# A gated-linear-attention encoder layer: the first sweep reads its tokens from a transposed copy of the input, and the norm factor of each token is multiplied in behind the matrix products

## The chip, the cores and the metric

The kernel runs on one NeuronCore of a Trainium2 chip. The metric is the device time of one execution in microseconds (us). Five engines work from queues of their own, each strictly in order: TensorE (PE in the profile; PEld is its weight load), VectorE (DVE), ScalarE (ACT), GpSimd (POOL) and SyncE (SP), which here only issues DMA transfers. They wait for each other through semaphores.

## The reference

With 2048 tokens of width 1024 and depth 1, one layer is computed: a norm over the tokens, a gated linear attention (GLA) mixer, a residual, a second norm, a feed-forward part with a short convolution, a residual, and a last norm. What the change touches is the first line and the projection behind it:

```python
def rms_normalize(x):
    y = xf * lax.rsqrt(jnp.mean(xf * xf, axis=-1, keepdims=True) + EPS)
...
h = rmsnorm(x, mix_norm_w[i])          # rms_normalize(x) * w
...
proj = h @ w_in                        # 1024 x 3088
q, k, v, r, glr = jnp.split(proj, ...)
log_a = jax.nn.log_sigmoid(glr @ w_gate2 + b_gate) / GLA_TAU
...                                    # scan over chunks of 64 tokens
o = rms_normalize(o) * norm_w * silu(r)
y = o @ w_out
x = x + y
x = x + conv_ffn(rmsnorm(x, ffn_norm_w), w_up, conv_w, conv_b, w_down)
return rmsnorm(x, final_norm_w)
```

The factor `rsqrt(mean(x*x) + EPS)` is one number for each token. A product `h @ w` is linear in the token's row, so this number can be applied to the row or to the result.

## The kernel before, in words

All large products run in float32 on PE as three matmuls of split operands (a high part, which ACT makes by a cast, and a low part, which DVE makes by a subtraction): `split` at L186, `mm3p` at L172. Products of 2x2 blocks are done with seven multiplications instead of eight (OPS, PORD at L81 to L83: p1, p5, p6, p2, p7, p3, p4 in the order in which they run). Tokens come in 16 tiles of 128; a unit takes two of them.

Four sweeps run over the eight units: R (the gate r of the mixer and the rank-16 decay gate), A and B (q, k, v of two heads each, and the scan), Y (the output projection). Then follow the two parts of the feed-forward stage. PE's time is filled by these one after the other; the first sweep, R, lasts until 228 us of the profiled span.

In sweep R the tokens must be normalised and transposed, since a matmul contracts over the partition dimension. `load_x` (L372) brings a tile of 128 tokens x 1024 into a ring of four raw buffers. `norm_x` (L379) squares it on ACT with a running sum (`rstd_of`, L204), takes the power -1/2 on POOL and multiplies the tile by this factor and the norm's weights on DVE (L383). `blocks_x` (L394) transposes the tile by eight PE matmuls with an identity (L401) into two PSUM banks and copies them to SBUF as blocks `hb` (L406; DVE, for tiles 2 and 3 ACT). `diff` makes the block differences `ht`. `prep_row` and `split_row` (L360, L426) split each of the seven operands and store it for the later sweeps (`h1d`).

`first_pair` (L908) does unit 0 by hand while weights still arrive: eight plain products (`product`, L1004) and the gate's small matmuls (`gate_plain`). `unit` (L1060) does the others. A unit's product p1 goes to a PSUM bank, ACT copies it out (`cp_R`, L1147), and p6, then p7 and p4 are accumulated onto the same bank; between them the partial sums are read out: p6 is copied like p1, p7 is added on DVE to the copy of p5 (L1091), and p4 is copied on ACT (L1163). So p6 can't begin before p1 is copied, p7 not before p6 is, p4 not before p7 is read. The decay gate's 32 rows (`gate_mm`, `gate_rows`) are multiplied by `w_gate2` with the bias as two further rows of ones (L567), and ACT takes softplus straight from PSUM (L569). `later_do` and `wevents` set the place of such work by a count of PE microseconds (`adv`). Behind this the framework orders each engine's instructions itself, so the order of a stream is not that of the source.

Of the kernel before, what the change touches and what calls it, by code (L numbers as in the profile page):

```python
# [16 lines left out]
P = 128  # L17
# [8 lines left out]
def hybrid_kernel(  # L26
    ctx: ExitStack,
    tc: tile.TileContext,
    x: bass.AP,
    mix_norm_w: bass.AP,  # L30
    ffn_norm_w: bass.AP,
# [340 lines left out]
    def load_x(t, name):  # L372
        xt = raw_tile([P, D], f"{name}_{t}")
        nc.sync.dma_start(xt, x[t * P:(t + 1) * P, :])
        return xt

    xin = {}

    def norm_x(t):  # L379
        xt = xin[t]  # L380
        junk = gp.tile([P, 1024], BF16, tag="cp", name=f"junk_{t}", bufs=4)
        rstd = rstd_of(xt, D, f"a{t}", junk, "a", nc.gpsimd if t < 4 else None)
        nc.vector.scalar_tensor_tensor(xt, xt, rstd, rp["nw"], op0=ALU.mult, op1=ALU.mult)  # L383

# [9 lines left out]
    def blocks_x(t):  # L394
        xt = xin.pop(t)
        bs = []
        for k in range(2):
            pt = aux_ps(f"pt_a{t}_{k}")
            for i in range(HK):
                kt = HK * k + i  # L400
                nc.tensor.transpose(pt[:, i * P:(i + 1) * P], xt[:, kt * P:(kt + 1) * P], ident)  # L401
# [4 lines left out]
            (nc.scalar.copy if t in (2, 3) else nc.vector.tensor_copy)(b, pt)  # L406
# [57 lines left out]
    def gate_weights():  # L464

        GR = 2 * RANK
        rp["wg"] = wg = rp["p"].tile([P, 2, KT, GR], F32R, name="wg")
        rp["wgx"] = wgx = rp["p"].tile([P, 2, KT, GR], F32R, name="wgx")
        graw = rp["p"].tile([P, 512], F32, tag="s2k", name="graw", bufs=SB)
        gv = graw[:, :KT * RANK].rearrange("p (a b) -> p a b", b=RANK)  # L470
        nc.sync.dma_start(gv, wv[:, :, OR + H * DV:OR + H * DV + RANK])
        nc.gpsimd.memset(f32(wg[:, 1, :, RANK:GR]), 0.0)
        nc.vector.tensor_copy(wg[:, 0, :, :RANK], gv)
        nc.vector.tensor_copy(wg[:, 1, :, :RANK], gv)
        nc.vector.tensor_sub(wg[:, 0, :, RANK:GR], gv, f32(wg[:, 0, :, :RANK]))
        nc.gpsimd.memset(f32(wgx[:, 1, :, RANK:GR]), 0.0)

        def others():

            gx_ = graw[:, KT * RANK:2 * KT * RANK].rearrange("p (a b) -> p a b", b=RANK)  # L480
            nc.vector.tensor_add(gx_[:, :HK], gv[:, :HK], gv[:, HK:])
            nc.vector.tensor_scalar(gx_[:, HK:], gv[:, :HK], -1.0, 0.0, op0=ALU.mult, op1=ALU.add)
            nc.vector.tensor_copy(wgx[:, 0, :, :RANK], gx_)
            nc.vector.tensor_copy(wgx[:, 1, :, :RANK], gx_)
            nc.vector.tensor_sub(wgx[:, 0, :, RANK:GR], gx_, f32(wgx[:, 0, :, :RANK]))

        later_do(24.0, others)

    def gate_weights2():
# [4 lines left out]
        for i in range(6):  # L494
            nc.sync.dma_start(w2raw[i * RANK:(i + 1) * RANK, :], w_gate2)
        for i in range(2):
            nc.sync.dma_start(w2raw[96 + i:97 + i, :], b_gate)
        def parts():
            nc.vector.tensor_copy(w2s[0:98, :], w2raw[0:98, :])
            for r in (slice(64, 96), slice(96, 98)):  # L500
                nc.vector.tensor_sub(w2s[r, :], w2raw[r, :], f32(w2s[r, :]))
            nc.vector.tensor_copy(w2s[96:97, :], w2raw[96:97, :])

        later_do(44.0, parts)
        rp["gstk"] = rp["p"].tile([P, T], F32R, name="gstk")
        nc.gpsimd.memset(f32(rp["gstk"][96:98, :]), 1.0)

# [49 lines left out]
    def gates(b, t0, t1, t2):  # L557
# [6 lines left out]
        def softplus(half):  # L564
            for tt in (2 * half, 2 * half + 1):
                pz = aux_ps(f"pz_{b}_{tt}")
                nc.tensor.matmul(pz, rp["gstk"][0:98, tt * P:(tt + 1) * P], rp["w2s"][0:98, :], start=True, stop=True)  # L567
                e = s2k(f"e_{b}_{tt}")
                nc.scalar.activation(e, pz, AF.Softplus, scale=-1.0)  # L569
                es.append(e)  # L570
# [339 lines left out]
    def first_pair():  # L910
# [42 lines left out]
        def weight(slot, ij, key=None):  # L953
# [50 lines left out]
        def product(i, jj, k):  # L1004
# [6 lines left out]
            if jj == 1:  # L1011
                t = out_tile(f"o{i}{k}_{ps_}_{j}")
                nc.scalar.copy(t, bank[i, k])
                nc.sync.dma_start(rd[k][i], t)
# [16 lines left out]
        need_raw[0, 1] = a12  # L1031
        product(1, 0, 0)
        norm_x(2)
        norm_x(3)
        product(1, 0, 1)
        weight("p2", (0, 1), "p2")
        product(1, 1, 0)
        gate_plain(j, 1, 0, *h[1, 0])
        blocks_x(2)
        blocks_x(3)  # L1040
        product(1, 1, 1)
        gate_plain(j, 1, 1, *h[1, 1])
        done["rows"] = len(PORD)
        prep_rows(len(PORD) + 1)
        sum5()
        product(0, 1, 0)
        prep_rows(len(PORD) + 2)
        sum6()
        product(0, 1, 1)
        later_do(22.0, diffs)  # L1050
        for t in (4, 5):
            xin[t] = load_x(t, "x")
        heapq.heappush(wevents, (clock["now"] + 1.0, next(seq), sum7))
# [10 lines left out]
    def unit(ps_, j):  # L1064
# [15 lines left out]
        if ps_ == "R":  # L1080
            if j + 2 < NP:
                for t in (e + 4, d + 4):
                    xin[t] = load_x(t, "x")
            if j + 1 < NP:
                for i, t in enumerate((e + 2, d + 2)):
                    norm_x(t)
                    later_do(TX[i], lambda t=t: blocks_x(t))

        def out(src, other, name):
            t = out_tile(f"{name}_{ps_}_{j}")  # L1090
            add(t, src, other)  # L1091
            return t
# [5 lines left out]
        for i, o in enumerate(PORD):  # L1098
# [46 lines left out]
            if o in ("p1", "p5", "p6"):  # L1145
                keep[o] = cp_tile(f"c{o}_{ps_}_{j}")
                nc.scalar.copy(keep[o], a)  # L1147
            elif o == "p2":
                o11 = out(a, keep["p1"], "o11")
            elif o == "p7":  # L1150
                o22 = out(a, keep["p5"], "o22")
            elif o == "p3":
                o12 = out(a, keep["p6"], "o12")
            if ps_ == "R":
# [6 lines left out]
                elif o == "p4":  # L1161
                    o21 = out_tile(f"o21_{ps_}_{j}")
                    nc.scalar.copy(o21, a)  # L1163
                    nc.sync.dma_start(rd[e][1], o21)
            else:
# [11 lines left out]
                elif o == "p4":  # L1177
                    scan[n]["v"] = scan_v(g, e, a)
                scan_slot(4 * i + 4)
# [263 lines left out]
    rp["h"] = rp["hctx"].enter_context(tc.tile_pool(name="rh", bufs=1, side="right"))  # L1443
    xin[0] = load_x(0, "x")
    rp["nw"] = rp["h"].tile([P, D], F32, name="nw_mix")
    nc.sync.dma_start(rp["nw"], mix_norm_w.partition_broadcast(P))
    xin[1] = load_x(1, "x")
    first_pair()
# [94 lines left out]
_INS = [  # L1543
    "x", "mix_norm_w", "ffn_norm_w", "final_norm_w",
    "gla_w_in", "gla_w_gate2", "gla_b_gate", "gla_norm_w", "gla_w_out",
# [26 lines left out]
```

## Time and profile before

| | us |
|---|---|
| time, median of 3 runs | 2183.61 (2178.07 to 2184.76) |
| span of the profiled execution (first to last instruction) | 2176.4 |
| sweep R in that span, to the first product of sweep A | 0 to 228.4 |
| the two feed-forward stages | 852 to 2176.4 |

The page gives the span of the profiled execution and no time beside it; what lies around a span (7.2 us from the median's side) is taken as the same before and after. A row of the profile names a line, an engine, an operation and its tiles (output <- inputs), then a count, the busy time, the mean time of one in ns and the idle time before it. A row of a timeline gives start, duration, engine, line and operation.

### The profile page before, as it was taken

What the parts mean: (1) busy time and instruction counts of PE and PEld (TensorE: products, weight loads), DVE (VectorE), ACT (ScalarE), POOL (GpSimd) and SP (SyncE); (2) the same over time, 40 slices, a digit from 0 to 9 for tenths busy, and PEclk for the clock granted to TensorE, in tenths of its full rate; (3) what the DMA queues carried; (4) which work ended last, traced back from release to release, by engine and by line L of the source; (5) the groups of instructions that cost most, each with busy time, mean ns of one, the idle gap of its engine ahead of it and who ended that gap; (6) DMA issues with size and microseconds to landing.
All of it is one profiled execution on the core that took longest, in us unless ns stands there. A gap on an engine that the chain in (4) does not pass through costs nothing.

```text
span 2176.4 us, 28914 instructions
## 1 busy us (share of the span) xinstructions
PE 2086.0 (96%) x9832; PEld 1730.6 (80%) x9832; DVE 1648.3 (76%) x2168; ACT 1104.3 (51%) x2024; POOL 734.9 (34%) x606
## 2 busy tenths in 40 slices
PE   7999999989998999799999998999999999999998
PEld 5788788878887887677888777888888877888886
DVE  8756888798888663778899776988888776457564
ACT  5555756665565775444554453554445533333342
POOL 2000011111111002456666554666565444037010
PEclk9999999999999999999999999999999999999999
DMA  6646684578557999654453458242424567254453
GB/s 219 223 165 211 213 297 137 159 229 298 178 195 251 323 344 365 207 163 131 146 184 102 146 177 291 88 131 76 139 77 124 187 247 269 97 184 160 141 182 113
DMA packets 305124, 411.76 MB, mean 189 GB/s; under 512 B 23742, under 2 KB 160110, under 8 KB 304976
## 3 DMA queue, kind: packets, MB, share of 16 engines
q1 hardware_dynamic: 267440, 346.99, 48.2%
q10 hardware_dynamic: 37536, 62.93, 8.6%
q8 instruction: 77, 1.26, 0.2%
q14 instruction: 71, 0.58, 0.1%
HBM read 266.70 MB, written 143.13 MB: 188 GB/s over the span
## 4 chain that ended last, share of the span: by engine, by line
PE 65%; DVE 13%; DMA 10%; issue 6%; ACT 2%; POOL 2%; SPq 0%; ACTq 0%; DVEq 0%; POOLq 0%
PE pd_p L180 5%; PE pd_p L181 5%; PE pd_p L179 5%; PE ua L179 5%; PE ua L180 5%; PE ua L181 5%; DVE t L1255 4%; DMA h_p<-hd_p 2%; PE uc L179 2%; PE uc L181 2%; PE uc L180 2%; PE mp_Y L180 2%; PE mp_Y L181 2%; PE mp_Y L179 2%; PE mp_R L179 2%
## 5 line engine op out<-in xcount | busy, mean ns | idle before, releaser
L179 PE MATMUL ua<-h_p,uw_p 128*128 128x512 f32 x704 | 279.0, 396 | 28.0 <-ACT c L1237 23.2
L1255 DVE SCALAR_TENSOR_TENSOR t<-u,cw,t 128x1024 f32<-128x1024 f32 x176 | 270.4, 1542 | 10.3 <-ACT t L1253 9.1
L180 PE MATMUL ua<-h_p,uw_p 128*128 128x512 f32 x704 | 277.7, 394 | 0.0
L181 PE MATMUL ua<-h_p,uw_p 128*128 128x512 f32 x704 | 277.2, 394 | 0.0
L180 PE MATMUL pd_p<-dw_p,da 128*128 128x512 f32 x616 | 240.7, 391 | 3.4 <-DVE da L189 3.4
L181 PE MATMUL pd_p<-dw_p,da 128*128 128x512 f32 x616 | 240.3, 390 | 0.0
L179 PE MATMUL pd_p<-dw_p,da 128*128 128x512 f32 x616 | 240.1, 390 | 0.0
L189 DVE TENSOR_TENSOR da<-da_p,da 128x512 fp32r<-128x512 f32 x154 | 131.4, 906 | 105.4 <-ACT da L188 105.3
L189 DVE TENSOR_TENSOR uw_p<-ur,uw_p 128x512 fp32r<-128x512 f32 x176 | 168.6, 979 | 48.8 <-ACT uw_p L188 48.4
L188 ACT CAST da<-da_p 128x512 fp32r<-128x512 f32 x154 | 85.3, 619 | 207.9 <-PE pd_p L181 149.9
L179 PEld LDWEIGHTS ua<-h_p,uw_p 128*128 128x128 f32 x704 | 134.4, 191 | 59.6 <-ACT c L1237 31.8
L188 ACT CAST uw_p<-us 128x512 fp32r<-128x512 f32 x132 | 82.1, 622 | 169.0 <-POOL us L1217 130.7
L189 DVE TENSOR_TENSOR uw_p<-us,uw_p 128x512 fp32r<-128x512 f32 x132 | 127.9, 978 | 47.8 <-ACT uw_p L188 46.8
L181 PEld LDWEIGHTS ua<-h_p,uw_p 128*128 128x128 f32 x704 | 134.5, 191 | 28.6
L180 PEld LDWEIGHTS ua<-h_p,uw_p 128*128 128x128 f32 x704 | 134.5, 191 | 27.9
L180 PEld LDWEIGHTS pd_p<-dw_p,da 128*128 128x128 f32 x616 | 116.0, 188 | 28.7 <-DVE da L189 4.7
L179 PE MATMUL uc<-h_p,uw_p 128*128 128x512 f32 x352 | 137.2, 390 | 0.9 <-DVE u L1328 0.9
L679 POOL TENSOR_TENSOR r<-r,gnw 128x512 f32<-128x512 f32 x32 | 46.9, 1466 | 268.6 <-ACT r L678 228.2
L181 PE MATMUL uc<-h_p,uw_p 128*128 128x512 f32 x352 | 136.9, 389 | 0.0
L180 PE MATMUL uc<-h_p,uw_p 128*128 128x512 f32 x352 | 136.9, 389 | 0.0
L181 PEld LDWEIGHTS pd_p<-dw_p,da 128*128 128x128 f32 x616 | 116.1, 188 | 24.1
L179 PEld LDWEIGHTS pd_p<-dw_p,da 128*128 128x128 f32 x616 | 116.1, 188 | 24.0
(278 smaller groups left out, 5474.8 us busy)
## 6 DMA issues: line engine op xcount, KB each, us to landing
ur<-in_ffn_w_up_dram SPq DMA_DIRECT2D x168, 256.0 KB, 3.7
da_p<-ad_p SPq DMA_DIRECT2D x154, 256.0 KB, 3.8
h_p<-hd_p SPq DMA_DIRECT2D x56, 512.0 KB, 8.0
ad_p<-as_p SPq DMA_DIRECT2D x88, 256.0 KB, 2.3
ad_p<-t SPq DMA_DIRECT2D x66, 256.0 KB, 3.1
x<-in_x_dram SPq DMA_DIRECT2D x32, 512.0 KB, 4.7
ch<-in_ffn_w_down_dram SPq DMA_DIRECT2D x61, 256.0 KB, 4.2
hr_A_p<-h1d_p SPq DMA_DIRECT2D x56, 256.0 KB, 3.0
```

What stands on the lines that cost most here:

```text
L179: nc.tensor.matmul(ps_ap, ah, bl, start=(first and i == 0), stop=False, **kw)
L180: nc.tensor.matmul(ps_ap, al, bh, start=False, stop=False, **kw)
L181: nc.tensor.matmul(ps_ap, ah, bh, start=False, stop=(last and i == len(pairs) - 1), **kw)
L188: nc.scalar.copy(hi, src)
L189: nc.vector.tensor_sub(lo, src, f32(hi))
L679: nc.gpsimd.tensor_mul(r, r, sp["gnw"])
L1255: nc.vector.scalar_tensor_tensor(t, u[:, k:k + TS], cw[:, k, c:c + 1], t, op0=ALU.mult, op1=ALU.add)
```

## The change

Two inputs are laid out anew on the host: `xt` holds the input tile by tile with the features on the partitions (each of 16 tiles is 128 x 2 x 512), and the norm's weights come as 128 x 8, so that feature kt*128+p lies on partition p. The blocks `hb` are now xt times the weight, one DVE multiply of 128 x 512 each with the weight broadcast along the tokens; the PE transposes, their PSUM banks and the copies out of them are gone, and so is the row norm `norm_x`.

The factor of each token goes to the result. Its square sum is taken from the rows of `x`, which are loaded once more, in halves of 128 x 512, into a single buffer `xr`: `squares` squares a half in place on ACT; then comes the load of the next half into the same buffer. After the second half POOL adds, scales and takes the power into `rs`, 128 x 16. Where a product leaves PSUM, a copy becomes an ACT activation with `rs` as its scale, an add becomes a DVE scalar_tensor_tensor, in the sweeps R, A and B. The gate's softplus is preceded by a DVE instruction that multiplies by `rs` and adds the broadcast bias `bg`; ACT then works on SBUF.

```diff
+    def load_xt(t, n=1):
+        r = raw_tile([P, 2, 512], f"xt_{t}")
+        for i in range(n):
+            ks = slice(2 * i // n, 2 * (i + 1) // n)
+            nc.sync.dma_start(r[:, ks, :], xt[t][:, ks, :])
+        return r
...
-    def norm_x(t):
-        xt = xin[t]
-        junk = gp.tile([P, 1024], BF16, tag="cp", name=f"junk_{t}", bufs=4)
-        rstd = rstd_of(xt, D, f"a{t}", junk, "a", nc.gpsimd if t < 4 else None)
-        nc.vector.scalar_tensor_tensor(xt, xt, rstd, rp["nw"], op0=ALU.mult, op1=ALU.mult)
+    def load_rows(t, i):
+        xrow[t, i] = rp["h"].tile([P, 512], F32, tag="xr", name=f"xr_{t}_{i}", bufs=1)
+        nc.sync.dma_start(xrow[t, i], x[t * P:(t + 1) * P, 512 * i:512 * (i + 1)])
...
+    def squares(t, i):
+        r = xrow.pop((t, i))
+        if i == 0:
+            sq[t] = small("ssq", f"ssq_a{t}", 2, "a")
+        nc.scalar.activation(r, r, AF.Square, accum_out=sq[t][:, i:i + 1])
+        if i == 1:
+            ssq = sq.pop(t)
+            var = small("var", f"var_a{t}", kind="a")
+            nc.gpsimd.tensor_add(var, ssq[:, 0:1], ssq[:, 1:2])
+            nc.gpsimd.tensor_scalar(var, var, 1.0 / D, EPS, op0=ALU.mult, op1=ALU.add)
+            nc.gpsimd.tensor_tensor(rs[:, t:t + 1], var, neghalf, op=ALU.pow)
...
         for k in range(2):
-            pt = aux_ps(f"pt_a{t}_{k}")
-            for i in range(HK):
-                kt = HK * k + i
-                nc.tensor.transpose(pt[:, i * P:(i + 1) * P], xt[:, kt * P:(kt + 1) * P], ident)
...
-            (nc.scalar.copy if t in (2, 3) else nc.vector.tensor_copy)(b, pt)
+            w = nwt[:, HK * k:HK * (k + 1)].unsqueeze(2).to_broadcast([P, HK, P])
+            nc.vector.tensor_tensor(b.rearrange("p (a c) -> p a c", c=P), xb[:, k, :].rearrange("p (a c) -> p a c", c=P), w, op=ALU.mult)
...
-                nc.tensor.matmul(pz, rp["gstk"][0:98, tt * P:(tt + 1) * P], rp["w2s"][0:98, :], start=True, stop=True)
+                nc.tensor.matmul(pz, rp["gstk"][0:96, tt * P:(tt + 1) * P], rp["w2s"][0:96, :], start=True, stop=True)
                 e = s2k(f"e_{b}_{tt}")
-                nc.scalar.activation(e, pz, AF.Softplus, scale=-1.0)
+                n = b * NT + tt
+                nc.vector.scalar_tensor_tensor(e, pz, rs[:, n:n + 1], rp["bg"], op0=ALU.mult, op1=ALU.add)
+                nc.scalar.activation(e, e, AF.Softplus, scale=-1.0)
...
+            nc.scalar.activation(vh, v, AF.Identity, scale=scale)
+            nc.vector.scalar_tensor_tensor(vl, v, scale, f32(vh), op0=ALU.mult, op1=ALU.subtract)
...
         fetch((0, 0))
+        xin[1] = load_xt(1, 2)
+        fetch((1, 0))
         gate_weights()
+        load_rows(0, 0)
         gate_weights2()
-        fetch((1, 0))
-        xin[2], xin[3] = load_x(2, "x"), load_x(3, "x")
         fetch((1, 1))
+        xin[2], xin[3] = load_xt(2), load_xt(3)
...
             if j + 1 < NP:
+                halves_ = [(t, i) for t in (e + 2, d + 2) for i in range(2)]
+                load_rows(*halves_[0])
+                def next_rows(n):
+                    squares(*halves_[n])
+                    if n < 3:
+                        load_rows(*halves_[n + 1])
+                for n in range(4):
+                    later_do(TSQ * (n + 1), lambda n=n: next_rows(n))
                 for i, t in enumerate((e + 2, d + 2)):
-                    norm_x(t)
                     later_do(TX[i], lambda t=t: blocks_x(t))
...
-            add(t, src, other)
+            nc.vector.scalar_tensor_tensor(t, src, rs[:, t_:t_ + 1], other, op0=ALU.mult, op1=ALU.add)
...
-                nc.scalar.copy(keep[o], a)
+                t_ = e if o == "p1" else d
+                nc.scalar.activation(keep[o], a, AF.Identity, scale=rs[:, t_:t_ + 1])
...
-                    nc.scalar.copy(o21, a)
+                    nc.scalar.activation(o21, a, AF.Identity, scale=rs[:, e:e + 1])
...
+    laid["xt"] = inputs["x"].reshape(16, 128, 2, 4, 128).transpose(0, 4, 2, 3, 1).reshape(16, 128, 2, 512)
+    laid["mix_norm_w"] = inputs["mix_norm_w"].reshape(8, 128).T
```

In `first_pair` eight calls of `next_rows` are spread between the products, and `product` copies its bank with `rs[:, k:k + 1]` as scale. TSQ is 4.8. The gate weights move to the pool that also holds `hb` and `xr`.

The change moves instructions on every engine. On PE, behind product p2 of unit 1 (`mp_R`; `pg` is the decay gate's bank), the order before is

```order
L181 MATMUL mp_R_980<-w_R_p_727,h_R_p_934 128x512
L401 MATMUL pt_a_0_993<-ident,x_869 128x128 x4
L401 MATMUL pt_a_1_1000<-ident,x_869 128x128 x4
L539 MATMUL pg_923<-h_R_p_934,wg 32x128
L540 MATMUL pg_923<-h_R_p_934,wg 32x128
```

and the order now is

```order
L181 MATMUL mp_R_944<-w_R_p_694,h_R_p_894 128x512
L182 MATMUL mp_R_944<-w_R_p_694,h_R_p_894 128x512
L183 MATMUL mp_R_944<-w_R_p_694,h_R_p_894 128x512
L560 MATMUL pg_883<-h_R_p_894,wg 32x128
L561 MATMUL pg_883<-h_R_p_894,wg 32x128
```

The eight transposes are gone there, as at all other places; nothing else of PE's order changes in sweep R but one matmul at its very start.

On ACT, in unit 3, from the copy of p1 (`cp_R_1484`, then those of p5 and p6) to the first row operand of unit 4, the order before is

```order
L1147 COPY cp_R_1484<-mp_R_1456 128x512
L188 CAST h_R_p_1505<-ht_p_1326 128x512
L1147 COPY cp_R_1503<-mp_R_1490 128x512
L188 CAST h_R_p_1523<-hb_1_1320 128x512
L1147 COPY cp_R_1521<-mp_R_1456 128x512
L188 CAST h_R_p_1566<-hb_1_1272 128x512
L208 ACTIVATE junk_1666,ssq_a_1667<-x_1432 128x1024
L208 ACTIVATE junk_1674,ssq_a_1675<-x_1434 128x1024
L188 CAST h_R_p_1613<-hb_0_1545 128x512
```

and now, over the same stretch,

```order
L1198 ACTIVATE cp_R_1418<-mp_R_1390,rs 128x512
L403 ACTIVATE xr_0_1600,ssq_a_1664<-xr_0_1600 128x512
L190 CAST h_R_p_1443<-ht_p_1265 128x512
L403 ACTIVATE xr_1_1666,ssq_a_1664<-xr_1_1666 128x512
L1198 ACTIVATE cp_R_1441<-mp_R_1424,rs 128x512
L190 CAST h_R_p_1461<-hb_1_1259 128x512
L1198 ACTIVATE cp_R_1459<-mp_R_1390,rs 128x512
L190 CAST h_R_p_1501<-hb_1_1221 128x512
L403 ACTIVATE xr_0_1711,ssq_a_1781<-xr_0_1711 128x512
L403 ACTIVATE xr_1_1783,ssq_a_1781<-xr_1_1783 128x512
L190 CAST h_R_p_1542<-hb_0_1485 128x512
```

Four squares of halves (L403) stand here, two of them ahead of the copies of p5 and p6. Counted over the whole stream of the changed kernel, squares 1 to 7 stand ahead of the copy of p1 in unit 1, 8 to 13 between there and that of unit 2, 14 to 20 up to that of unit 3, 21 to 27 up to that of unit 4; the 32nd and last stands ahead of the second row operand of unit 5.

On SP, which issues the loads of these halves (`xr`), the order now, around the 20th to 23rd of them, is

```order
L394 DMA xr_1_1529<-in_x_dram 128x512
L614 DMA ed_153<-e_3_1155 128x512
L1215 DMA rd_1_175<-o_R_1377 128x512
L394 DMA xr_0_1600<-in_x_dram 128x512
L369 DMA h1d_p_121<-hb_1_1221 128x512
L369 DMA h1d_p_123<-ht_p_1518 128x512
L394 DMA xr_1_1666<-in_x_dram 128x512
L369 DMA h1d_p_124<-ht_p_1520 128x512
L394 DMA xr_0_1711<-in_x_dram 128x512
```

The loads stand between stores of unit 2's results (`rd`), of gate factors (`ed`) and of row operands (`h1d`), each of which waits for the engine that makes it.

More of the change, by code (lines that the diff above doesn't have):

```diff
@@ L75, in hybrid_kernel @@
     TX = (10.8, 13.5)
+    TSQ = 4.8
     TS = 1024
@@ L200, in hybrid_kernel @@
     lastrow = cst.tile([P, 1], F32, name="lastrow")
+    rs = cst.tile([P, NTT], F32, name="rs")
+    nwt = cst.tile([P, KT], F32, name="nwt")
     def small(tag, name, n=1, kind=""):
@@ L466, in gate_weights @@
         GR = 2 * RANK
-        rp["wg"] = wg = rp["p"].tile([P, 2, KT, GR], F32R, name="wg")
-        rp["wgx"] = wgx = rp["p"].tile([P, 2, KT, GR], F32R, name="wgx")
+        rp["wg"] = wg = rp["h"].tile([P, 2, KT, GR], F32R, name="wg")
+        rp["wgx"] = wgx = rp["h"].tile([P, 2, KT, GR], F32R, name="wgx")
         graw = rp["p"].tile([P, 512], F32, tag="s2k", name="graw", bufs=SB)
@@ L495, in gate_weights2 @@
             nc.sync.dma_start(w2raw[i * RANK:(i + 1) * RANK, :], w_gate2)
-        for i in range(2):
-            nc.sync.dma_start(w2raw[96 + i:97 + i, :], b_gate)
+        rp["bg"] = rp["p"].tile([P, 512], F32, name="bg")
+        nc.sync.dma_start(rp["bg"], b_gate.partition_broadcast(P))
         def parts():
[L499 to L502, printed above, removed]
+            nc.vector.tensor_copy(w2s[0:96, :], w2raw[0:96, :])
+            nc.vector.tensor_sub(w2s[64:96, :], w2raw[64:96, :], f32(w2s[64:96, :]))
         later_do(44.0, parts)
         rp["gstk"] = rp["p"].tile([P, T], F32R, name="gstk")
-        nc.gpsimd.memset(f32(rp["gstk"][96:98, :]), 1.0)
     def gate_plain(j, i, c, hh, hl):
@@ L641, in scan_e, with scan_v @@
         return e
-    def scan_v(g, t, v):
+    def scan_v(g, t, v, scale=None):
         vh = sp["a"].tile([P, 512], F32R, tag=f"vh{t % 2}", name=f"vh_{g}_{t}", bufs=1 + t % 2)
         vl = sp["a"].tile([P, 512], F32R, tag=f"vl{t % 2}", name=f"vl_{g}_{t}", bufs=1 + t % 2)
-        split(vh, vl, v)
+        if scale is None:
+            split(vh, vl, v)
+        else:
+            nc.scalar.activation(vh, v, AF.Identity, scale=scale)
+            nc.vector.scalar_tensor_tensor(vl, v, scale, f32(vh), op0=ALU.mult, op1=ALU.subtract)
         return vh, vl
@@ L961, in weight, with next_rows @@
                 ready.add((ps_, key))
+        halves_ = [(t, i) for t in range(4) for i in range(2)]
+        def next_rows():
+            squares(*halves_.pop(0))
+            if halves_:
+                load_rows(*halves_[0])
         V = [(slice(None), slice(2 * k, 2 * k + 2)) for k in range(2)]
@@ L1012, in product @@
                 t = out_tile(f"o{i}{k}_{ps_}_{j}")
-                nc.scalar.copy(t, bank[i, k])
+                nc.scalar.activation(t, bank[i, k], AF.Identity, scale=rs[:, k:k + 1])
                 nc.sync.dma_start(rd[k][i], t)
@@ L1031, in first_pair @@
         need_raw[0, 1] = a12
+        next_rows()
         product(1, 0, 0)
-        norm_x(2)
-        norm_x(3)
+        next_rows()
         product(1, 0, 1)
+        next_rows()
         weight("p2", (0, 1), "p2")
+        next_rows()
         product(1, 1, 0)
@@ L1048, in first_pair @@
         sum6()
+        next_rows()
         product(0, 1, 1)
+        next_rows()
         later_do(22.0, diffs)
         for t in (4, 5):
-            xin[t] = load_x(t, "x")
+            xin[t] = load_xt(t)
         heapq.heappush(wevents, (clock["now"] + 1.0, next(seq), sum7))
@@ L1082, in unit, with out @@
                 for t in (e + 4, d + 4):
-                    xin[t] = load_x(t, "x")
+                    xin[t] = load_xt(t)
             if j + 1 < NP:
+                halves_ = [(t, i) for t in (e + 2, d + 2) for i in range(2)]
+                load_rows(*halves_[0])
+                def next_rows(n):
[4 more added lines that the diff above has]
+                    later_do(TSQ * (n + 1), lambda n=n: next_rows(n))
                 for i, t in enumerate((e + 2, d + 2)):
-                    norm_x(t)
                     later_do(TX[i], lambda t=t: blocks_x(t))
-        def out(src, other, name):
+        def out(src, other, name, t_):
             t = out_tile(f"{name}_{ps_}_{j}")
-            add(t, src, other)
+            nc.vector.scalar_tensor_tensor(t, src, rs[:, t_:t_ + 1], other, op0=ALU.mult, op1=ALU.add)
             return t
@@ L1146, in unit @@
                 keep[o] = cp_tile(f"c{o}_{ps_}_{j}")
-                nc.scalar.copy(keep[o], a)
+                t_ = e if o == "p1" else d
+                nc.scalar.activation(keep[o], a, AF.Identity, scale=rs[:, t_:t_ + 1])
             elif o == "p2":
-                o11 = out(a, keep["p1"], "o11")
+                o11 = out(a, keep["p1"], "o11", e)
             elif o == "p7":
-                o22 = out(a, keep["p5"], "o22")
+                o22 = out(a, keep["p5"], "o22", d)
             elif o == "p3":
-                o12 = out(a, keep["p6"], "o12")
+                o12 = out(a, keep["p6"], "o12", d)
             if ps_ == "R":
@@ L1443, in hybrid_kernel @@
     rp["h"] = rp["hctx"].enter_context(tc.tile_pool(name="rh", bufs=1, side="right"))
[L1444 to L1447, printed above, removed]
+    nc.sync.dma_start(nwt, mix_norm_w)
+    xin[0] = load_xt(0, 2)
     first_pair()
```

20 lines of the change are left out of this document (13 added, 7 removed).

## The prediction

> **What bounds the kernel now.** I read the page's head and its chain first, then busy time by stretches, then PE's waits inside sweep R, since all else is left as it was but for the read-outs of A and B.
>
> ```profile
> span 2176.4 us, 28914 instructions
> PE 65%; DVE 13%; DMA 10%; issue 6%; ACT 2%; POOL 2%; SPq 0%; ACTq 0%; DVEq 0%; POOLq 0%
> 0.00:18.82 18.82, 3.76 (x17) 3.23 (x17) 8.60 (x15) 8.78 (x12) 4.38 (x20) 0.98 0.81 266
> 18.82:47.70 28.88, 28.56 (x144) 23.44 (x145) 28.71 (x38) 18.69 (x30) 7.32 (x5) 0.90 0.64 218
> 47.70:228.40 180.70, 175.25 (x997) 145.11 (x996) 123.12 (x182) 99.71 (x177) 7.86 (x12) 1.00 0.59 200
> ```
>
> The three stretches are the start, unit 0 and units 1 to 7 of sweep R; the columns are length, busy time of PE, weight load, DVE, ACT and POOL, granted clock, DMA share and GB/s. From 18.82 on PE is the bound, with DVE beside it in unit 0 (28.71 of 28.88). What is taken from PE there is time, unless something becomes later than PE. ACT has room: 99.71 of 180.70.
>
> **What goes away.** The transposes, and what they cost on PE:
>
> ```profile
> L401 PE MATMUL pt_a<-ident,x 128*128 128x128 f32 x96 | 12.4, 272 | 0.0
> 36.66 1.48 PE L401 MATMUL pt_a<-ident,x 128*128 128x128 f32 x12
> 38.87 0.48 PE L179 MATMUL m_R<-w_R_p,h_R 128*128 128x512 f32 x1
> 61.55 1.03 PE L401 MATMUL pt_a<-ident,x 128*128 128x128 f32 x8
> 62.34 0.30 PE L539 MATMUL pg<-h_R_p,wg 128*32 128x128 f32 x1
> PE mp_R L179 <- ACT h_R_p L188: 1.5, 1, 1.5
> 71.75 0.68 DVE L1091 TENSOR_TENSOR o_R<-mp_R,cp_R 128x512 f32<-128x512 f32 x1
> ```
>
> The 272 ns of one overlap, so I count by starts: eight hold PE from 61.55 to 62.34, 0.79 us, and I take 0.82 with the refill behind them; a unit has sixteen, 1.65. Units 1 to 6 have them (96), 9.9 us together. In unit 0 sixteen hold PE from 36.66 to 38.87: 2.2 us. One wait of 1.5 us goes too: the row names ACT, but p4 of unit 1 needs p7 read out, and that read (71.75 to 72.43) was late on DVE behind row norms and copies that are gone.
>
> The start: before, the second matmul of the first product waits for DVE until 18.82.
>
> ```profile
> 4.64 1.06 ACT L208 ACTIVATE junk<-x 128x1024 bf16<-128x1024 f32 x1 [2.06 <-DMA x<-in_x_dram]
> 8.16 1.06 ACT L208 ACTIVATE junk<-x 128x1024 bf16<-128x1024 f32 x1 [2.37 <-DMA x<-in_x_dram]
> 11.16 1.05 ACT L188 CAST w_R_p<-ws_p 128x1024 fp32r<-128x1024 f32 x1 [0.65 <-DMA ws_p<-in_gla_w_in_dram]
> 18.82 0.80 PE L180 MATMUL m_R<-w_R_p,h_R 128*128 128x512 f32 x1 [2.50 <-DVE h_R L189]
> ```
>
> These landings give the supply: 1.5 MB (x, norm weights, x) by 8.16, 2.5 MB by 11.16, about 0.33 MB a us. Now four blocks come before DVE reaches the multiplies: its order has a sum that waits for the third weight block, and the gate weights, which now queue behind the fourth. 3 MB are in at about 12.7, the gate weights at 13.1; casts, four multiplies at 0.6 and one subtraction end at 17.1. So the start is 1.7 us earlier, no more. Without anything new in the way the sum is 1.7 + 2.2 + 9.9 + 1.5 = 15.3 us.
>
> **What is added beside PE's work.** DVE, which was full in unit 0, pays 32 multiplies of 128x512 and saves 28 copies and 16 row norms:
>
> ```profile
> L383 DVE SCALAR_TENSOR_TENSOR x<-x,rstd_a,nw_mix 128x1024 f32<-128x1024 f32 x12 | 15.3, 1283 | 7.0 <-POOL rstd_a L212 7.0
> L406 DVE COPY hb<-pt_a 128x512 f32<-128x512 f32 x24 | 15.4, 682 | 0.0
> L390 DVE TENSOR_TENSOR ht_p<-hb,hb 128x512 f32<-128x512 f32 x12 | 8.2, 683 | 0.0
> ```
>
> A multiply with a broadcast operand is in no row; the difference ht of the same size (683 ns) is nearest and I take it. In units 1 to 7 it equals the copy, so 15.3 us of norms are saved and 16 gate instructions of 0.68 (10.9) come in. In unit 0 DVE gets four multiplies (2.7) for two norms (2.6): no change. The bounds, half and double of 683 ns, move DVE by 11 us down or 22 up over a sweep in which it had 57 us of room: nothing. The scale by rs in the read-outs: ACT copies of 588 ns against some 610 for an activation (interpolated below), DVE adds of 680 with one scalar more; 85 to 96 of a kind, over sweeps in which both engines have room, so nothing on the path, and less than 0.1 us where a bank waits for one.
>
> **The new wait.** The rows of x come through one buffer. A load on SP waits for the square before it, the square for its load, and squares stand in ACT's order ahead of copies that PE waits for. So ACT can't pass a square before its load landed, and 32 of them follow each other.
>
> ```profile
> L723 ACT ACTIVATE og<-po 128x256 f32<-128x256 f32 x64 | 24.0, 381 | 22.0 <-PE po L181 18.6 <-DMA ws_B_p<-wm_B 3.5
> L208 ACT ACTIVATE junk<-x 128x1024 bf16<-128x1024 f32 x16 | 16.9, 1057 | 5.6 <-DMA x<-in_x_dram 5.4
> L208 ACT ACTIVATION_READ_ACCUMULATOR junk<-x 128x1 f32 x16 | 3.0, 189 | 0.0
> hr_A_p<-h1d_p SPq DMA_DIRECT2D x56, 256.0 KB, 3.0
> da_p<-ad_p SPq DMA_DIRECT2D x154, 256.0 KB, 3.8
> x<-in_x_dram SPq DMA_DIRECT2D x32, 512.0 KB, 4.7
> DMA to landing us min/median/max: 2.5/3.1/5.4
> ```
>
> Between 381 ns for 256 columns and 1057 for 1024 a square of 512 takes 0.61, with its read-out 0.7 (they overlap by 0.1). The last row is that of the tile r, 30 loads of 256 KB in sweeps A and B. A load of 256 KB in rows of 2 KB so takes from 2.5 (the least of these) to 4.7 (x, twice the size); hr_A is the same shape from SP, so I take its median, 3.0. One turn is 3.7 us.
>
> [...]
>
> Where the chain stands in unit 0: the second square is behind the cast of a late weight block (25.09 before; its load now goes out behind later casts), done at about 30; the fourth behind a cast that waits for DVE's sums, 39; the fifth behind a read-out that needs the factor of tile 1, that is three POOL instructions. In this stretch POOL is slow beside DVE:
>
> ```profile
> 21.10 3.10 POOL L210 TENSOR_SCALAR var_a<-ssq_a 128x1 f32<-128x1 f32 x1 [8.81 <-ACT junk L208]
> 26.48 0.45 POOL L210 TENSOR_SCALAR var_a<-ssq_a 128x1 f32<-128x1 f32 x1
> 27.02 1.53 POOL L212 TENSOR_TENSOR rstd_a<-var_a,neghalf 128x1 f32<-128x1 f32 x1
> ```
>
> 0.45 to 3.10 each, I take 1 each, 3 together: 42, then a read-out and casts, the fifth at 45, and three more turns with a cast or two bring the eighth to about 57 (54 to 60). Unit 1 then starts near 46, not at 47.7 less 5, and its p6 waits about as before.
>
> From the eighth square to the 27th are 19 turns, 70.3 us. Four places are longer: the ninth behind copies that need the factor of tile 3, 1.05; a stretch of seven ACT instructions (4.3 us) before the 15th, 1.25; the load of the 17th behind the store of a gate factor, 1.95; that of the 18th likewise, 0.6: 4.9 in all. So the 27th ends at 57 + 70.3 + 4.9 = 132.2. Behind it stand, ahead of p6 in unit 4:
>
> ```profile
> L569 ACT ACT_TABLE_LOAD x4 | 5.1, 1283 | 0.1
> L569 ACT ACTIVATE e<-pz 128x512 f32<-128x512 f32 x16 | 8.7, 598 | 0.3
> L1147 ACT COPY cp_R<-mp_R 128x512 f32<-128x512 f32 x21 | 12.4, 588 | 15.3 <-PE mp_R L181 14.7 <-issue 0.6
> 133.39 0.59 ACT L1147 COPY cp_R<-mp_R 128x512 f32<-128x512 f32 x1 [0.19 <-PE mp_R L181]
> ```
>
> A table load, two softplus and the copy: 1.3 + 1.2 + 0.6 = 3.1, so p6 starts at 135.3. Before, p5 of unit 4 has ended at 133.4 (the last row) and p6 follows at once. The change is therefore 1.9 us **behind** at that point: all that PE saved by then, some 10 us, is waited away. Behind it only five squares are left, and no copy of the next units stands behind one that is late; the transposes of units 4, 5 and 6 are then a plain gain, 3 x 1.65 = 4.95. Net: 3.05 us earlier at the end of R.
>
> Against the profiled execution's own time this is 2176.4 - 3.05; what lies around the span stays, so from the median 2183.6 I get **2180.6**. Sweeps A, B and what follows keep their order but for a few neighbours that change places, and I count nothing there.
>
> **The rivals.** (1) The loads are quick, at 2.5 us: a turn of 3.2 takes 9.5 us off the 19, the 27th square ends at 122.7, and the gain is 12.5: 2171.1; near the 15.3 of the ceiling. For it: loads of r have reached it, and sweep R's DMA share is only 0.59. Against it: the median of these loads is 3.1. [...] (2) Slower: the loads take 3.8, as da_p of the same size does. A turn is then 4.5, p6 of unit 4 starts 15.2 later, 12.2 us behind before at the end: 2195.8. It decides from a load of 3.16 on (no gain) and is a loss of more than 6.5 us from 3.5 on. For it: R gets 8 MB more to load, and SP's order puts stores that wait ahead of loads. Against it: hr_A at 3.0. With 4.7 it would be 17 more. (3) The change does not do what it says, because DVE in unit 0 or POOL's three instructions hold the start: each us of the eighth square is a us of the end; 60 instead of 57 gives 2183.6, no change.
>
> **How the numbers follow.** A measurement of this kernel can tell about 0.3%, 6.5 us, from no change. The forecast holds for loads from 2.8 to 3.4 us, that is from 3.8 us better to 7.6 worse than 2180.6: 0.42. Rival 1 has 0.32, rival 2 0.20, rival 3 0.06. Faster by over 0.3% (below 2177.1): rival 1 and a part of the forecast, 0.38. Slower (above 2190.1): rival 2 and a little, 0.21. Within: 0.41. The range reaches to 2169, past rival 1, and to 2194, most of rival 2.
>
> **What would show it.** In the new trace pt_a is gone from PE, and R ends some 3 us earlier, not 15. L403 on ACT should have its idle time put down to the DMA of xr, some 1.5 to 2.5 us a square; the distance from one square to the next in units 2 and 3 should be 3.7 us or a little more; PE should wait for the copy of p1 (now L1198) in units 2 to 4 and not in 5 to 7. Landing of xr near 3.0. If xr lands by 2.6, or the squares are waited for less than 1 us, rival 1 holds; if units 2 to 4 last 3 us or more longer than the 25.8 of before (180.7 over seven), rival 2. The start is right if the first product runs from about 17, and unit 0 ends before 45. The forecast is wrong as a whole if PE's waits in R go to another engine than ACT.

## The result, and the profile after

The changed kernel takes 2200.86 us (median of 4 runs, 2199.84 to 2202.14), the kernel before 2180.84 on the same chip (2175.41 to 2184.76): a ratio of 1.0101, 95% interval 1.0083 to 1.0120. It is slower by 1%. The forecast was 2180.6, and the range ended at 2194. The profiled execution's span is 22.0 us longer. One of the ten executions of a later run, the second with two buffers, took 8915 us; its ratio leaves that one out.

The page of the changed kernel, its head and the chain that ended last:

```profile
span 2198.4 us, 28729 instructions
PE 60%; DVE 15%; DMA 12%; issue 5%; ACT 4%; POOL 2%; SPq 1%; ACTq 0%; DVEq 0%; POOLq 0%
PE pd_p L182 6%; PE pd_p L183 6%; PE pd_p L181 6%; PE ua L181 5%; PE ua L183 5%; PE ua L182 5%; DVE t L1306 4%; DMA xr<-in_x_dram 4%; PE uc L181 2%; PE uc L182 2%; PE uc L183 2%; PE mp_Y L182 2%; PE mp_Y L183 2%; PE mp_Y L181 2%; DVE uw_p L191 2%
```

PE's share of that chain fell from 65% to 60%, and a row stands in it that is new: the loads of the row halves, `xr`, with 4%. Busy time in the same three stretches as in the prediction (start, unit 0, units 1 to 7 of sweep R; length, PE, weight load, DVE, ACT, POOL, granted clock, DMA share, GB/s):

```profile
0.00:17.45 17.45, 0.80 (x1) 0.29 (x1) 8.04 (x14) 7.36 (x10) 1.91 (x15) 1.00 0.80 229
17.45:43.71 26.26, 26.25 (x127) 21.19 (x128) 23.59 (x33) 12.77 (x19) 10.68 (x6) 1.00 0.80 284
43.71:244.80 201.09, 178.10 (x902) 141.64 (x901) 122.86 (x176) 109.28 (x215) 18.97 (x43) 0.94 0.66 217
```

Unit 1 starts at 43.71 instead of 47.70, which is the gain forecast for the start and unit 0. Then units 1 to 7 take 201.1 us instead of 180.7, at a granted clock of 0.94 instead of 1.00, though PE has 95 instructions fewer. Sweep R ends 16.4 us late. By the last product of each stage, sweep A adds 0.8, B 5.9, Y takes 1.9 back, and the rest adds 0.8: 22.0 in all.

What PE waits for from 43 to 245 us (waiting instruction, releaser, sum, times, longest):

```profile
PE pe L603 <- ACT e L612: 8.4, 8, 2.2
PE mp_R L181 <- ACT cp_R L1198: 7.3, 4, 2.9
PE mp_R L181 <- DVE o_R L1141: 4.8, 2, 2.6
PE pg L560 <- ACT gstk L573: 2.4, 1, 2.4
```

And the same in units 1 to 7 of the kernel before:

```profile
PE mp_R L179 <- ACT cp_R L1147: 3.8, 2, 2.1
PE mp_R L179 <- ACT h_R_p L188: 1.5, 1, 1.5
PE mp_R L179 <- DVE o_R L1091: 0.2, 1, 0.2
```

23.0 us of waits against 5.5. The row on `cp_R` is the one that the prediction spoke of; those on `e` (the gate's exponential, with `pe` its transpose on PE) and on `gstk` were not in it. All of ACT's stand in one stream behind squares. The squares themselves, by the view of the tile `xr`:

```profile
L403 ACT ACTIVATE xr<-xr x32: 623/632/636, 15.2 to 167.6; 128x512 f32<-128x512 f32 x32
  DMA xr<-in_x_dram: 51.4, 26
DMA to landing us min/median/max: 2.5/3.5/5.0
```

ACT sits 51.4 us idle before 26 of the 32, until a load lands; the median landing is 3.5 us (over the 14 loads whose landing the trace has). A piece of ACT's timeline (start, duration, operation, idle time before) with the 27th square and what stands behind it:

```profile
146.36 0.63 ACT L403 ACTIVATE xr<-xr 128x512 f32<-128x512 f32 x1 [2.31 <-DMA xr<-in_x_dram]
146.90 0.19 ACT L403 ACTIVATION_READ_ACCUMULATOR xr<-xr 128x1 f32 x1
147.11 1.28 ACT L592 ACT_TABLE_LOAD   x1
148.40 1.15 ACT L592 ACTIVATE e<-e 128x512 f32<-128x512 f32 x2
149.46 0.67 ACT L1198 ACTIVATE cp_R<-mp_R,rs 128x512 f32<-128x512 f32 x1
```

The order is as forecast, square, table load, two softplus, copy. But the square ends at 147.1, not 132.2.

PE's timeline shows something more. Behind the wait for `gstk` the matmuls of 512 columns start 0.43 us apart, later 0.23:

```profile
49.00 0.25 PE L560 MATMUL pg<-h_R_p,wg 128*32 128x128 f32 x1 [2.41 <-ACT gstk L573]
...
51.16 0.63 PE L181 MATMUL mp_R<-w_R_p,h_R_p 128*128 128x512 f32 x1
51.59 0.63 PE L182 MATMUL mp_R<-w_R_p,h_R_p 128*128 128x512 f32 x1
...
53.09 0.39 PE L183 MATMUL mp_R<-w_R_p,h_R_p 128*128 128x512 f32 x1
53.32 0.40 PE L181 MATMUL mp_R<-w_R_p,h_R_p 128*128 128x512 f32 x1
```

That is half clock for some 3 us (the granted clock is 0.50 from 49.7 to 52.8). With the distances between starts summed over PE's timeline from the start of unit 1 to the end of R, less the waits, the 20.4 us of those units come apart:

| units 1 to 7 of sweep R, us | before | after |
|---|---|---|
| 588 products `mp_R` | 138.0 | 149.4 |
| waits that the rows name | 5.5 | 23.0 |
| transposes `pt_a` | 9.7 | none |
| gate matmuls and the rest of PE | 27.5 | 28.8 |
| sum | 180.7 | 201.1 |

The same 588 products take 11.4 us longer.

### The profile page after: what moved, and what is told of

Read it like the earlier page. It is cut to its first block, busy times and chain, and to the rows that moved or that the text cites. A ratio compares the mean times of both kernels' runs of the same rounds, so it can differ in the third digit from the quotient of the medians.

```text
span 2198.4 us, 28729 instructions
## 1 busy us (share of the span) xinstructions
PE 2091.3 (95%) x9704; PEld 1720.1 (78%) x9704; DVE 1625.2 (74%) x2158; ACT 1115.5 (51%) x2052; POOL 742.5 (34%) x633
## 4 chain that ended last, share of the span: by engine, by line
PE 60%; DVE 15%; DMA 12%; issue 5%; ACT 4%; POOL 2%; SPq 1%; ACTq 0%; DVEq 0%; POOLq 0%
PE pd_p L182 6%; PE pd_p L183 6%; PE pd_p L181 6%; PE ua L181 5%; PE ua L183 5%; PE ua L182 5%; DVE t L1306 4%; DMA xr<-in_x_dram 4%; PE uc L181 2%; PE uc L182 2%; PE uc L183 2%; PE mp_Y L182 2%; PE mp_Y L183 2%; PE mp_Y L181 2%; DVE uw_p L191 2%
## 5 line engine op out<-in xcount | busy, mean ns | idle before, releaser
L1306 DVE SCALAR_TENSOR_TENSOR t<-u,cw,t 128x1024 f32<-128x1024 f32 x176 | 261.8, 1493 | 10.8 <-ACT t L1304 9.3
L191 DVE TENSOR_TENSOR uw_p<-ur,uw_p 128x512 fp32r<-128x512 f32 x176 | 161.5, 934 | 67.2 <-ACT uw_p L190 67.0
L191 DVE TENSOR_TENSOR uw_p<-us,uw_p 128x512 fp32r<-128x512 f32 x132 | 121.5, 930 | 52.3 <-ACT uw_p L190 51.2
```

The source lines that it names most:

```text
L191: nc.vector.tensor_sub(lo, src, f32(hi))
L1306: nc.vector.scalar_tensor_tensor(t, u[:, k:k + TS], cw[:, k, c:c + 1], t, op0=ALU.mult, op1=ALU.add)
```

## The experiments

The theory after this: ACT's stream stops at each square until the single buffer has been loaded; PE's waits, on whatever ACT makes, follow from it, and PE then runs at half clock for a while. Rivals: S, the longer softplus path and the scaled read-outs make the waits; Q, the squares' own time; L, loads that are slow whatever the order. The numbers below are medians, with the ratio to the kernel before on the same chip and its 95% interval; ends of R and of other stages are those of the profiled execution. Such an execution lay up to 7.4 us from the median of its kernel, so a few us between two ends of R are not firm.

**No rows at all.**

```diff
+    nc.gpsimd.memset(rs, 1.0)
     def load_rows(t, i):
-        xrow[t, i] = ...
+        return
     def squares(t, i):
-        r = xrow.pop((t, i))
-        ...
+        return
```

> Leaves out the norm factor of the mixer: rs is set to 1 once, the 32 loads of xr and their 32 squares are gone; all read-outs, the softplus path and the order of the rest stay. Chain theory (squares in ACT's order wait for the loads of the single buffer, PE waits behind them, and PE then runs some us at half clock): the 23 us of PE waits in units 1 to 7 and the 11 us of half clock nearly go, sweep R ends at 210 to 218 instead of 244.8, the time is 2166 to 2176. Rival S (the longer softplus path and the read-outs scaled by rs make the waits): the 8.4 us in which PE waits for e stay with their half clock, R ends at 230 or later, the time is 2186 or more.

2168.81 us, 0.9963 (0.9952 to 0.9974). R ends at 212.1; units 1 to 7 last 169.6 us, with 4.5 us of waits, 1.7 of them for `e`. Rival S falls for sweep R: the read-outs and the softplus are those of the changed kernel. R is 16.3 us shorter than before, so the ceiling of 15.3 in the prediction was right. The whole is only 7.5 shorter than before; sweep B has 5.5 of the rest (below).

**Squares without loads.**

```diff
-        xrow[t, i] = rp["h"].tile([P, 512], F32, tag="xr", name=f"xr_{t}_{i}", bufs=1)
-        nc.sync.dma_start(xrow[t, i], x[t * P:(t + 1) * P, 512 * i:512 * (i + 1)])
+        if not xrow:                         # the first half row stays
+            ...
```

> Leaves out 31 of the 32 loads of rows: one half row stays in SBUF and is squared 32 times, so the factor is that of 512 numbers of other tokens; squares, POOL's three instructions and rs stay. Chain theory: only waiting for loads costs, so this is within 5 us of the run without rows, 2166 to 2180. Rival Q (the squares' own 26 us on ACT and POOL's chain to rs cost it): near the changed kernel, 2190 to 2200.

2171.88, 0.9982 (0.9970 to 0.9994). R ends at 215.4, 3.3 us behind the run without rows; the waits are 5.7 us. So the squares' own time does not make the 32.7 us by which R ends later in the changed kernel than without rows, and Q falls as their cause: it is the loads ahead of them. One thing is left open: with no load to wait for (and a result tile of their own) the squares also moved, 20 of them ahead of the copy of p1 in unit 1, and the last is done at 63.8. What they would cost at their places in the changed kernel this run does not show; the paced run with two buffers, below, bounds it for four a unit.

**Two buffers.**

```diff
-... tag="xr", name=f"xr_{t}_{i}", bufs=1)
+... tag="xr", name=f"xr_{t}_{i}", bufs=2)
                 load_rows(*halves_[0])
+                load_rows(*halves_[1])
...
-                    if n < 3:
-                        load_rows(*halves_[n + 1])
+                    if n < 2:
+                        load_rows(*halves_[n + 2])
...
-        return gp.tile([P, 512], F32, tag="cp", name=name, bufs=4)
+        return gp.tile([P, 512], F32, tag="cp", name=name, bufs=3)
```

> xr gets two buffers, each load is issued one square earlier; the ring of copies has three buffers instead of four to make room. Nothing is left out. [...] Chain theory with the framework's order: two buffers let the squares move still further ahead in ACT's order (ten, not seven, ahead of the copy of p1 in unit 1), so ACT still waits for loads; two are in flight, a square each 2.5 us instead of 4.6, and the waits gather in units 1 to 3: 2178 to 2192.

2229.09, 1.0239 (1.0221 to 1.0256), not the 2178 to 2192 expected: R ends at 231.2, 13.6 earlier than in the changed kernel, but the up-projection stage is 45.5 us longer. PE's waits after R in this run:

```profile
PE ua L181 <- ACT c L1290: 38.6, 20, 11.4
```

and in the changed kernel:

```profile
PE ua L181 <- ACT c L1288: 24.3, 8, 6.5
```

`c` is taken from the ring that I had shortened to make room. So that ring got its fourth buffer back and the room was taken elsewhere, with the rest of the edit as before:

```diff
-    SB = 8
+    SB = 7
```

> Two buffers for xr with the square in place, as in the first run of that kind, but the ring of copies keeps its four buffers, and room comes from s2k (seven instead of eight). Nothing is left out. In the first run the up-projection stage was 46 us longer than in the changed kernel, which I put down to the ring of three that this stage also uses; so here that stage is back at 880 to 890 us. R: squares run ahead in ACT's order as there, so R ends at 228 to 236, and the time is 2180 to 2190. If two buffers are enough: R ends by 220, 2172 to 2178.

2187.20, 1.0040 (1.0024 to 1.0056). The up-projection is back at 890 us (886 in the changed kernel), so it was the ring. R ends at 233.6. The framework orders ACT's stream by its own reckoning, and with two buffers it put ten squares, not seven, ahead of the copy of p1 in unit 1; the last square is done at 127.0, not 168.4. The wait before squares moved forward rather than went (that row of `xr` in this run):

```profile
  DMA xr<-in_x_dram: 31.9, 15
```

Two buffers alone give a third of the loss in R back: 11.2 of the 32.7 us between the changed kernel and the one without rows.

**Paced squares**, one buffer.

```diff
-        nc.scalar.activation(r, r, AF.Square, accum_out=sq[t][:, i:i + 1])
+        nc.scalar.activation(cp_tile(f"junk_{t}_{i}"), r, AF.Square, accum_out=sq[t][:, i:i + 1])
```

> One line: the square writes into the ring of four buffers that also holds the copies of p1, p5 and p6, not back into xr. Nothing is left out. The ring ties the squares to the units: four a unit stand in ACT's order, not six or seven, and each load is issued well before its square. Chain theory: ACT's wait for xr falls from 51 us to under 15, R ends at 212 to 222, the time is 2170 to 2180. Rival L (the loads are slow because the DMA queues are full, whatever the order): ACT still waits over 35 us for xr, R ends after 238, the time is over 2193. Rival S as before: PE's 8.4 us for e stay, time over 2186.

2189.87, 1.0067 (1.0052 to 1.0082). Four squares a unit now stand in the stream, and R ends at 234.4: better than the changed kernel by 10, worse than expected by 12. ACT still waits 30.8 us for `xr`, now at 16 places:

```profile
  DMA xr<-in_x_dram: 30.8, 16
DMA to landing us min/median/max: 2.5/3.0/5.9
```

Of a unit's four squares two or three stand close behind each other in the stream, and there the single buffer is as late as ever (waits of 2.1 and 3.6 us ahead of the two at 121.4 and 126.3).

**Paced squares and two buffers** (both edits, SB = 7).

> The square writes into the ring of copies (four buffers, as in the paced run), and xr has two buffers with each load issued one square earlier; the ring s2k of the gate's tiles has seven buffers instead of eight to make room. Nothing is left out. Chain theory: with the squares held to four a unit and a load ahead, ACT waits under 12 us for xr (paced with one buffer: 30.8), PE's waits in units 1 to 7 fall to 6 to 10 us, R ends at 216 to 224, the time is 2172 to 2182. If the loads themselves are the limit: R's end stays near the 234 of the paced run, 2186 or more.

2177.55, 1.0000 (0.9981 to 1.0019). ACT's wait for `xr`, and the landings:

```profile
  DMA xr<-in_x_dram: 9.0, 6
DMA to landing us min/median/max: 2.5/3.6/9.2
```

PE's waits in units 1 to 7 are 9.7 us. R ends at 223.0, 21.8 us earlier than in the changed kernel, with landings no quicker than its 3.5. So it is the order and the buffer that make a landing cost time, not the landing as such: L falls. R is still 10.9 us behind the run without rows; squares four a unit, what ACT still waits for loads, and the way to the factor cost no more than that together.

**The first factor.** In the changed kernel POOL's first add for `rs` reads two columns of 128x1 and lasts 9 us, beside a DVE that runs one two-input instruction after the other:

```profile
30.33 9.04 POOL L407 TENSOR_TENSOR var_a<-ssq_a 128x1 f32<-128x1 f32 x1 [27.58 <-ACT xr L403]
```

```diff
         blocks_x(3)
+        gap = cst.tile([P, P], F32R, name="gap")
+        for _ in range(8):
+            nc.vector.tensor_copy(gap, b[0, 0][:, :P])
```

> The changed kernel with eight extra DVE casts of 128x128 (one input each, into a tile that nobody reads) in unit 0, which the framework sets between the DVE instructions with two inputs there. In the changed kernel POOL's first add of 128x1 lasts from 30.33 to 39.37 us, while DVE runs instructions with two inputs back to back until 39.09, and the first read-out waits for rs until 40.33. If POOL is shut out by DVE's second input: the add ends within one or two DVE instructions (under 4 us), rs of tile 0 is there by 33 to 37, and the first read-out (L1048) starts before 38. If the long add has another cause: it lasts 8 to 9 us again, and the read-out starts at 40 or later. The time of the whole stays within 6 us of the changed kernel's, since the chain of squares decides later.

2194.16, 1.0080 (1.0056 to 1.0105). The same add in this run, and the first read-out on ACT:

```profile
30.66 1.10 POOL L407 TENSOR_TENSOR var_a<-ssq_a 128x1 f32<-128x1 f32 x1 [27.92 <-ACT xr L403]
```

```profile
36.94 0.67 ACT L1048 ACTIVATE o_R<-m_R,rs 128x512 f32<-128x512 f32 x1
```

The read-out comes at 36.9 instead of 40.3, and the eighth square ends at 57.8 instead of 60.1, R at 237.5. More DVE work made the kernel no slower (a ratio of 1.0080 against 1.0101). Of the 7.3 us by which R ends earlier only 2.3 come from the eighth square; the 19 turns behind it took 81.7 us instead of 87.1, and why is not shown. The add took 1.10 us beside this stream of DVE and 9.04 beside the other, so what DVE runs bears on it; which property of DVE's instructions decides is not shown, since the add ended at 31.76 and the casts there ran at 29.76 and 33.37.

The same wait can be avoided by an earlier second load, on top of the paced run with two buffers, where this line stood behind the loads of the next blocks:

```diff
         gate_weights2()
+        load_rows(0, 1)
         fetch((1, 1))
```

> The paced run with two buffers, and the load of the second half row is issued ahead of the last weight block of the start, not behind two blocks of the input. Nothing is left out. So the second square stands before DVE's dense stretch in unit 0, POOL makes the first factor by about 22 us instead of 40.9, and ACT's wait of 5.5 us for it goes. R then ends at 216 to 221 (223.0 without), the time is 2169 to 2177, faster than before by 0 to 0.4%. If that wait was hidden behind PE: R ends at 223 again.

2177.76, 1.0007 (0.9995 to 1.0019). R ends at 220.3, as expected, but the time is not the 2169 to 2177 expected, and no gain can be told from it. Sweep R is now 8.2 us shorter than in the kernel before, and sweep B 7.6 us longer.

**Sweep B.** On top of the run without rows:

```diff
-            nc.vector.scalar_tensor_tensor(t, src, rs[:, t_:t_ + 1], other, op0=ALU.mult, op1=ALU.add)
+            if ps_ == "R": nc.vector.scalar_tensor_tensor(...)
+            else: add(t, src, other)
...
-                scan[n]["v"] = scan_v(g, e, a, rs[:, e:e + 1])
+                scan[n]["v"] = scan_v(g, e, a)
```

and the copies of p1, p5 and p6 likewise.

> As the run without rows (rs is 1, no loads, no squares), and sweeps A and B read their products out with plain copies and adds, without the factor; sweep R keeps its scaled read-outs. If the scaled read-outs cost sweep B its 5 us (224.6 against 219.1 before): B is back at 218 to 221 and the time is 4 to 7 below the run without rows, 2162 to 2166. If B is longer for another reason (the phase in which it starts, other neighbours): B stays at 223 to 226 and the time within 3 us of 2168.8.

2165.55, 0.9951 (0.9935 to 0.9967). Sweep B from first to last product, in the kernel before, in the run without rows, and here:

```profile
440.13:659.25 219.12, 212.71 (x1154) 181.29 (x1153) 190.81 (x361) 132.55 (x303) 35.49 (x33) 1.00 0.68 226
```

```profile
425.45:650.03 224.58, 215.12 (x1155) 184.70 (x1154) 196.71 (x363) 136.62 (x306) 35.77 (x33) 0.98 0.67 224
```

```profile
427.02:646.03 219.01, 212.71 (x1154) 181.36 (x1153) 191.93 (x361) 132.86 (x303) 36.47 (x33) 1.00 0.69 227
```

The scaled read-outs make this sweep 5.6 us longer, with 5 us more on DVE, which was at 87%, and 3.2 us more of waits on PE, one of them of 3.4. But the gain of the plain ones does not last: sweep Y takes 3.9 us more than in the run without rows, sweep A 0.7, R ends 0.9 later, and Y's last product starts at 840.8 against 841.0. So the 3.3 us between the two medians, whose intervals overlap, can't be put down to sweep B. Why Y gives back what B takes is not shown.

**Waits of known cause in the kernel before.**

```diff
                 nc.scalar.copy(keep[o], a)
+                if ps_ == "R" and o == "p1":
+                    for _ in range({2: 8, 3: 10, 4: 12, 5: 14, 6: 16}.get(j, 0)):
+                        nc.scalar.copy(keep[o], a)
```

> The kernel before, with the copy of p1 done again 8, 10, 12, 14 and 16 times in units 2 to 6 of sweep R (same values into the same tile), so that p6 waits for ACT by known lengths, some 1.5 to 6 us, with no new load and no other change. Clock theory: behind waits of some 2 us and more PE runs at half clock for 2 to 4 us and loses 1.3 to 2.8 us each time, so that R ends later by the waits (about 18 us in sum) and 6 to 12 us more. Rival: a wait costs its own length, R is later by the waits alone, within 2 us. [...]

2198.65, 1.0092 (1.0071 to 1.0113). The waits came out shorter than I had reckoned, the framework set other work between the copies: 14.1 us in units 1 to 7 against 5.5. The 588 products took 143.4 us against 138.0. One of the waits, with the slow stretch behind it:

```profile
177.85 0.50 PE L179 MATMUL mp_R<-w_R_p,h_R_p 128*128 128x512 f32 x1 [2.38 <-ACT cp_R L1150]
...
179.82 0.63 PE L179 MATMUL mp_R<-w_R_p,h_R_p 128*128 128x512 f32 x1
180.25 0.63 PE L180 MATMUL mp_R<-w_R_p,h_R_p 128*128 128x512 f32 x1
```

R ends 14.6 us later, for 8.6 us of waits: 5.4 are the products at half clock, 1.3 come from the rest of PE's work, and unit 1 started 0.7 earlier. (The whole is 20.0 us longer; sweep A has 5.8 of that, with 8.1 us of waits instead of 4.5, and this was not followed up.) Three waits were followed by it, of 2.73, 2.38 and 1.12 us (the last 2.6 us behind another of 1.86), each at a price of 1.6; four others, of 0.99 to 1.47 us, and that of 1.86 by itself were not. Such a stretch is mostly seven or eight products long, 0.43 us apart instead of 0.23; one in the changed kernel, behind the wait of 2.88 us at 87.9, has thirteen.

## Why the prediction was wrong

The forecast was a gain of 3.0 us, and the span grew by 22.0. The mechanism was the forecast one: ACT held at a square until its load lands, and PE held behind ACT. What failed were the size of a landing, the step that nothing is lost behind p6 of unit 4, and two costs that had been set to nothing: the slow stretch behind a wait, and the sweeps behind R. The 25.0 us between forecast and measurement are 3.0 at the eighth square, 9.5 in the landings, 2.4 in the rest of the turns, 4.5 behind p6 of unit 4 and 5.6 behind R; the slow stretches lie inside these. Point by point:

- **The start, 1.7 us, and the transposes of unit 0, 2.2.** Right as a sum: unit 1 starts at 43.7 instead of 47.7, a gain of 4.0 for 3.9. The parts are 1.4 and 2.6, so that the sum agrees so closely is in part luck.
- **The transposes of units 1 to 6, 9.9, and the ceiling of 15.3.** Right: 9.7 us of `pt_a` are gone, and the run without rows has R 16.3 us shorter.
- **The landing of 3.0 us.** This is the term of the sum that was mis-sized. It is 3.5. The 19 turns took 87.1 us (60.1 to 147.2) instead of 75.2: 9.5 of the 11.9 are the half us per landing, by this median, 2.4 the rest of a turn. The prediction had drawn the 3.0 from all loads of `hr_A`, most of which run in sweep A. The three in sweep R of the kernel before (47 to 160 us) landed in

```profile
hr_A_p<-h1d_p SPq DMA_DIRECT2D x3, 256.0 KB, 4.3
```

  so rows of the right sweep already pointed higher. Stores of `h1d` landed there in 2.0 us, and in the new R in 4.3 (43 to 170):

```profile
h1d_p<-hb SPq DMA_DIRECT2D x21, 256.0 KB, 2.0
```

```profile
h1d_p<-hb SPq DMA_DIRECT2D x22, 256.0 KB, 4.3
```

  The extra 8 MB were named as what speaks for rival 2. That they make the landings longer is not shown: in the run without rows, which lacks them, these stores take 2.9 (42 to 150), and in the paced run, which has them, the loads of `xr` land in 3.0.
- **The eighth square at 57.** 60.1. The fourth square was taken to stand ahead of the first read-out; it stands behind it, and that waits for POOL until 40.3. POOL's three instructions were put at 3 us and took 10; with the casts on DVE they took 3.2, and the eighth square ended at 57.8. This was rival 3's place, but it is 3 us of 15.
- **p6 of unit 4 at 135.3.** 150.2: 14.9 late, which is these two points, 3.0 and 11.9.
- **"Behind it only five squares are left ... a plain gain."** This step failed. PE was 16.8 us behind the kernel before at p6 of unit 4 (150.2 against 133.4), and 16.4 behind at the end of R: a gain of 0.4 for 4.95. The transposes behind that point do give 4.9; against them stand 4.1 us of waits, all for `e`, instead of 1.8, and 2.2 us more in products and gate matmuls. I had followed one consumer of ACT's stream, the copies, and not the gate's `e`, for which PE waits 8.4 us in all, from unit 2 on; in the run without rows 1.7 are left.
- **A wait costs its length.** So the sum was made, and it is not so: the known waits cost 14.6 us for 8.6. In the changed kernel the same products take 11.4 us longer. How much of that PE would have waited anyway, where the chain of loads is the bound, no run tells apart.
- **"Sweeps A, B and what follows keep their order ... I count nothing there."** Failed: 5.9 us in sweep B, of which 4.8 are left with A and Y at the end of Y, and 0.8 more behind it. The plain read-outs take 5.6 back in B, but not by the end of Y. "Nothing on the path" held in R, where DVE had 57 us of room, and not in B, where it had 28 of 219.

The forecast's own test said: if units 2 to 4 last 3 us or more longer than 25.8 each, rival 2 holds. They do: by their gate matmuls units 2 to 4 take 95.7 us (81.1 to 176.8), 32 each, against 78.0 before. Its mark for rival 1, a landing by 2.6, is a number that no run shows as a median: `xr` landed in 3.5 here, 2.5 at the least. Rival 2 at a landing of 3.5 gave 2190, a loss of 6.5; the eighth square, the rest of the turns, the gain that did not come behind p6 of unit 4 and the 5.6 behind R are what it lacks of 22.0. No version here beats both kernels by more than can be measured: the best that computes everything, 2177.55, is level with the one before.

## What to carry to other kernels

Ask of an instruction that waits for a load not only what waits for it, but what else stands behind it on its engine, and for how long that engine may stand still; the order and the number of buffers are two remedies, and here pacing and the second buffer were worth 10 and 11 us of sweep R alone and 22 together. Price a wait on PE with the slow stretch that can follow it (1.4 to 2.8 us each here), and take a landing from rows of the same sweep, with a range: a chain of many turns multiplies it, and the median landing of `xr` lay between 3.0 and 4.6 us in these runs. And where "free" work is added in several stages, look at the room of its engine in each of them.

## What the runs showed of the hardware that I had not expected

- In the changed kernel and in the run with known waits PE fell to half clock (products 0.43 us apart instead of 0.23), mostly for some 3 us and once for 5.6, behind some waits of 1.9 to 2.9 us and one of 1.12 close behind another, at 1.4 to 2.8 us each; others as long, of 1.79 in the changed kernel and 2.11 in the one before, cost only themselves.
- A POOL add of 128x1 lasted 9.04 us beside DVE's dense two-input stream and 1.10 with small one-input casts set into it. There it ended at 31.76, where one instruction with two inputs followed another (at 31.64), and the nearest casts ran at 29.76 and 33.37: what in the stream of DVE decides is not shown.
